# PSUM of a first stage shared out anew: three score buffers of two banks and two projection banks, for two and four

## The chip, the cores and the metric

The kernel runs on one core of a Trainium2 chip. The metric is the device time of one execution in microseconds (us), the median of several runs. All profile lines come from one profiled execution.

## What is computed

One layer reads x (4096 x 1024). A combined projection gives attention queries, a latent of 128 columns, indexer queries (8 heads of 32), indexer keys, head weights, gates, and the inputs of a state-space branch. The part that matters here is the choice of keys:

```python
idx_logits = jnp.einsum('bthd,bsd->bths', qi_b, ki)
index_score = jnp.einsum('bths,bth->bts', jax.nn.relu(idx_logits), wi_b)
index_score = jnp.where(causal[None], index_score, neg)
_, sel = lax.top_k(index_score, n_sel)          # n_sel = 256 of up to 4096 keys
```

Attention then runs over the chosen keys alone, the state-space branch is scanned, and both are gated, projected and normalised.

## The kernel before

The work falls into two halves. The **first stage** (lines 162 to 797) makes all projections and chooses the keys. The second (lines 801 to 1386: attention, state-space scan, output) needs the choice of all keys: a matmul (L1027) adds up a test over all groups, the result decides whether a slower selection has to run, and only then does attention begin.

In the first stage two kinds of work share the engines.

**Projections.** `prepare(c)` loads a chunk of 512 rows of x in eight tiles, transposes each with four PE instructions (L483) into a PSUM tile `ps_x`, and splits it in two (L85 on ACT, L87 on DVE; both read PSUM). `sweep(c, cols)` multiplies: one column block is 24 matmuls (eight triples, L98 to L100) into one `ps_x`, which ACT, or ACT and DVE, then drain. Indexer queries and keys need further short matmuls (L546, L547, L559 to L564), the keys and values of attention others; each takes a `ps_x` of its own. The weights of a sweep after the first are loaded by POOL's queue (L511).

**Selection.** The 30 query tiles that need a choice are taken in ten groups of two to five (`ORDER`); the last one is `[10, 11, 20, 21]`. `score(i)` makes the index scores of tile i: for each head, PE fills a `ps_i` of two banks with up to two matmuls (L254), ACT takes its relu into SBUF (L256), and DVE adds it with the head's weight to the tile's row of scores (L265). Then `select` searches a threshold in six or eight rounds. A round counts the scores above it, for some tiles on ACT (L325), for the others on DVE (L329), and is followed by 11 to 20 small DVE operations (L331 to L367). The first DVE operation of a group's rounds is L318, the first after them L372. Then each tile is cleaned up (L386 on ACT; L390, L391, the MAX8 of L393 and the MATCH_REPLACE8 of L401 on DVE) and its mask is written (L405). There are four large score buffers `acc`, so about two groups are in hand at once.

```python
165    psi = idxs.enter_context(tc.tile_pool(name="i_ps", bufs=2, space=PSUM))
251                    pi = psi.tile([P, 2 * C], FT, name="ps_i")
256                    ACT.activation(r[:, q0:q0 + m], pi[:, :m], AF.Relu)
457        pst = ph.enter_context(tc.tile_pool(name="p_t", bufs=4, space=PSUM))
481                ps = pst.tile([P, 4, P], FT, name="ps_x")
537                ps = pst.tile([P, C], FT, name="ps_x")
785        prepare(0)
786        for c in range(NCH):
787            sweep(c, range(3), None)
788            if c + 1 < NCH:
789                prepare(c + 1)
794        for g in ORDER:
795            select(g)
796        for c, following in zip((NCH - 1, *range(NCH - 1)), (*range(NCH - 1), None)):
797            sweep(c, range(3, len(COLS)), following)
```

PSUM has eight banks of 512 fp32 columns; `ps_i` takes two, `ps_x` one. So the program text has the three blocks one after the other, but it isn't the order in which they run: a scheduler with a model of the instructions' times orders each engine's queue when the program is built, and mixes projections of the last block (lines 796 and 797) in between the scores of the selection. Within a queue everything then runs in that fixed order: an instruction that waits holds up all behind it. In the second half the order on PE, DVE and ACT is written out by hand.

Of the kernel before, what the change touches and what calls it, by code (L numbers as in the profile page):

```python
# [27 lines left out]
PSUM = bass.MemoryType.PSUM  # L28
# [43 lines left out]
def tile_hymba(  # L72
# [89 lines left out]
    idxs = ctx.enter_context(ExitStack())  # L162
    one = idxs.enter_context(tc.tile_pool(name="i_one", bufs=1))
    wk = idxs.enter_context(tc.tile_pool(name="i_wk", bufs=2))
    psi = idxs.enter_context(tc.tile_pool(name="i_ps", bufs=2, space=PSUM))

    kst = one.tile([P, S], FR, name="kst")
    wi = one.tile([P, NT, HEADS], FT, name="wi")
# [284 lines left out]
    with ExitStack() as ph:  # L453
        xp = ph.enter_context(tc.tile_pool(name="p_x", bufs=1))
        wp = ph.enter_context(tc.tile_pool(name="p_w", bufs=WB))
        sm = ph.enter_context(tc.tile_pool(name="p_s", bufs=1))
        pst = ph.enter_context(tc.tile_pool(name="p_t", bufs=4, space=PSUM))

        selh = sm.tile([P, 4, P], FR, name="selh")
        sell = sm.tile([P, 4, P], FR, name="sell")  # L460
# [955 lines left out]
```

## Time and profile before

| | us |
|---|---|
| median of 3 runs (4113.29 to 4124.88) | 4118.75 |
| the profiled execution | 4111.49 |
| its span | 4109.7 |
| last score matmul of the selection starts (PE) | 1662.58 |
| the matmul that closes the first stage (L1027) | 1787.18 |

The rows below are of the profiled execution; times count from the start of its span. PEld is TensorE's weight load, PEclk the granted clock as a share of full speed. A wait is written as "who waited <- for whom".

### The profile page before, as it was taken

The page shows a single profiled execution, that of the slowest core. Times are in us where ns is not written, and L with a number is a line of the kernel's source. Part 1 is how long each engine was busy: PE and PEld are TensorE (multiplying, and loading weights), DVE is VectorE, ACT ScalarE, POOL GpSimd, SP SyncE. Part 2 cuts the span into 40 slices and gives each one's busy share as a digit, 9 for nine tenths or more (in the row PEclk, how much of TensorE's full clock was granted, in tenths as well). Part 3 has the DMA queues.
Part 4 walks back from the last instruction along what each step waited for, and adds up shares of the span by engine and source line. Part 5 has one row for each costly group of instructions (what it writes and reads, how often), then busy time and mean ns, then how long its engine had stood idle before and what let it go on. Part 6 is the DMA issues. An engine that isn't in the chain of part 4 may idle for free.

```text
span 4109.7 us, 64216 instructions
## 1 busy us (share of the span) xinstructions
PE 3683.6 (90%) x20925; PEld 3111.3 (76%) x20925; DVE 3298.1 (80%) x6879; ACT 2804.1 (68%) x4540; POOL 1545.4 (38%) x3405
## 2 busy tenths in 40 slices
PE   6788988988989989149999999999999999899998
PEld 5566766766757658038888898888898989788887
DVE  5898898888798888778888888888888889565554
ACT  4587878776767776647777777777777778534342
POOL 1110011111111111236665656666656542354543
PEclk9889989989989899569999999999999999999999
DMA  8766967767668677244545444444444444644441
GB/s 226 159 195 177 307 190 213 200 183 221 190 188 230 185 202 203 71 141 117 154 120 149 124 136 137 128 136 127 140 132 135 119 142 121 181 135 134 143 124 72
DMA packets 521898, 656.19 MB, mean 160 GB/s; under 512 B 126800, under 2 KB 367952, under 8 KB 521552
## 3 DMA queue, kind: packets, MB, share of 16 engines
q1 hardware_dynamic: 438800, 448.54, 37.7%
q0 software_dynamic: 82752, 203.45, 18.5%
q8 instruction: 167, 2.74, 0.3%
q14 instruction: 179, 1.47, 0.1%
HBM read 480.61 MB, written 169.13 MB: 158 GB/s over the span
## 4 chain that ended last, share of the span: by engine, by line
PE 45%; ACT 3%; DMA 3%; issue 2%; DVE 2%; POOL 2%; SPq 0%; ACTq 0%; POOLq 0%; DVEq 0%
PE ps_t L1149 10%; PE ps_o L1161 6%; PE ps_o L1162 5%; PE ps_s L1116 5%; PE ps_s L1117 5%; PE ps_y L99 2%; PE ps_y L98 2%; PE ps_y L100 2%; ACT sc L1132 2%; PE ps L959 2%; PE ps_g L99 1%; PE ps_g L100 1%; PE ps_g L98 1%; DMA mb<-mask_d 1%; ACT ph L85 1%
## 5 line engine op out<-in xcount | busy, mean ns | idle before, releaser
L87 DVE TENSOR_TENSOR pl<-ps_t,ph 128x512 fp32r<-128x512 f32 x1088 | 748.5, 689 | 194.2 <-ACT ph L85 181.1
L85 ACT ACTIVATE ph<-ps_t 128x512 fp32r<-128x512 f32 x1088 | 644.2, 596 | 372.6 <-PE ps_t L1149 353.8
L1119 DVE CUSTOM_DVE_ANT_0 sc<-ps_s,mb 128x512 f32<-128x512 f32 (+3 forms) x1152 | 725.6, 638 | 39.2 <-PE ps_s L1117 18.2
L1161 PE MATMUL ps_o<-ph,V 128*128 128x256 f32 x2176 | 659.3, 325 | 29.9 <-ACT ot L1165 27.0
L1149 PE MATMUL ps_t<-ident,sc 128*128 128x128 f32 x4352 | 655.7, 273 | 10.5 <-DVE pl L87 6.0
L256 ACT ACTIVATE relu<-ps_i 128x1024 f32<-128x1024 f32 (+5 forms) x624 | 534.6, 899 | 168.8 <-PE ps_i L254 147.2
L1132 ACT ACTIVATE sc<-sc,mx 128x1024 f32<-128x1024 f32 (+7 forms) x640 | 637.0, 997 | 7.3 <-DVE mx L1119 7.0
L1149 PEld LDWEIGHTS ps_t<-ident,sc 128*128 128x128 f32 x4352 | 537.0, 141 | 122.6 <-DVE pl L87 6.6
L265 DVE SCALAR_TENSOR_TENSOR acc<-relu,wi,acc 128x2048 f32<-128x2048 f32 (+15 forms) x322 | 558.1, 1733 | 77.2 <-ACT relu L256 74.3
L1162 PE MATMUL ps_o<-pl,V 128*128 128x256 f32 x2176 | 565.0, 282 | 2.6 <-DVE pl L87 2.6
L511 POOL DMA_DIRECT2D w<-w_d x294 | 159.0, 541 | 1085.9 <-PE ps_x L100 1005.8
L98 PE MATMUL ps_x<-xk,w 128*128 128x512 f32 x1280 | 517.1, 404 | 6.5 <-DVE st L87 2.0
L100 PE MATMUL ps_x<-xk,w 128*128 128x512 f32 x1280 | 507.3, 396 | 0.0
L99 PE MATMUL ps_x<-xk,w 128*128 128x512 f32 x1280 | 506.5, 396 | 0.0
L254 PE MATMUL ps_i<-kst,qst 128*128 128x512 f32 (+1 forms) x1136 | 394.9, 446 | 117.2 <-ACT relu L256 111.2
L1116 PE MATMUL ps_s<-KT,QH 128*128 128x512 f32 (+2 forms) x1152 | 438.2, 381 | 19.6 <-DMA V<-v_d 15.2
L1161 PEld LDWEIGHTS ps_o<-ph,V 128*128 128x128 f32 x2176 | 413.5, 190 | 47.4 <-ACT ot L1165 39.5
L1117 PE MATMUL ps_s<-KT,QL 128*128 128x512 f32 (+2 forms) x1152 | 436.4, 379 | 0.7 <-DVE QL L87 0.7
L1162 PEld LDWEIGHTS ps_o<-pl,V 128*128 128x128 f32 x2176 | 417.6, 192 | 7.3 <-DVE pl L87 3.3
L254 PEld LDWEIGHTS ps_i<-kst,qst 128*128 128x128 f32 x1136 | 222.1, 213 | 223.9 <-ACT relu L256 185.7
L325 ACT ACTIVATE junk_a<-acc,s_t 128x1920 int8<-128x1920 f32 (+14 forms) x152 | 333.1, 2191 | 53.8 <-DVE s_t L354 24.1
L98 PEld LDWEIGHTS ps_x<-xk,w 128*128 128x128 f32 x1280 | 245.7, 192 | 70.5 <-DMA w<-w_d 6.2
(408 smaller groups left out, 7435.4 us busy)
## 6 DMA issues: line engine op xcount, KB each, us to landing
w<-w_d POOLq DMA_DIRECT2D x294, 512.0 KB, 4.2
mb<-mask_d SPq DMA_DIRECT2D x416, 256.0 KB, 3.1
xs<-in_x_dram SPq DMA_DIRECT2D x120, 256.0 KB, 4.6
w_d<-w SPq DMA_DIRECT2D x42, 512.0 KB, 4.3
qs_d<-st SPq DMA_DIRECT2D x64, 256.0 KB, 3.0
k_d<-st SPq DMA_DIRECT2D x128, 128.0 KB, 2.4
v_d<-st SPq DMA_DIRECT2D x64, 256.0 KB, 3.5
QL<-qT_d SPq DMA_DIRECT2D x64, 256.0 KB, 4.2
```

The lines of the kernel that those rows point to most:

```text
L85: ACT.activation(hi, src, AF.Copy, scale=scale)
L87: DVE.tensor_tensor(lo, src, ft(hi), op=OP.subtract)
L98: PE.matmul(ps, lh, rh, start=first, stop=False)
L99: PE.matmul(ps, lh, rl, start=False, stop=False)
L100: PE.matmul(ps, ll, rh, start=False, stop=last)
L1116: PE.matmul(ps[:, :nn], QH[:, qs], kk, start=True, stop=False)
L1117: PE.matmul(ps[:, :nn], QL[:, qs], kk, start=False, stop=True)
L1119: DVE.tensor_tensor_reduce(self.sc[a][-1][:, o], ps[:, :n], self.mb[a][:, o], 1.0, TOP, OP.add, OP.min, mx[:, k:k + 1])
L1132: ACT.activation(v, v, AF.Exp, scale=-1.0, bias=nm, accum_out=self.ds[:, a, r:r + 1])
L1149: PE.transpose(pt[:, e, a, :], self.sc[a][r][:, o:o + P], ident)
L1161: PE.matmul(self.po, v, ph_[:, e, :], start=(b + e == 0), stop=False)
L1162: PE.matmul(self.po, v, pl_[:, e, :], start=False, stop=(b + e == self.nb - 1))
```

## The change

The pool of `ps_i` gets three buffers, and that of `ps_x` two. All eight banks are taken before (2 x 2 + 4) and after (3 x 2 + 2).

```diff
@@ -162,7 +162,7 @@
-    psi = idxs.enter_context(tc.tile_pool(name="i_ps", bufs=2, space=PSUM))
+    psi = idxs.enter_context(tc.tile_pool(name="i_ps", bufs=3, space=PSUM))
@@ -454,7 +454,7 @@
-        pst = ph.enter_context(tc.tile_pool(name="p_t", bufs=4, space=PSUM))
+        pst = ph.enter_context(tc.tile_pool(name="p_t", bufs=2, space=PSUM))
```

No instruction is added or removed, but the scheduler puts the first stage's queues in another order. Three places show it; `kst`, `qst`, `xk`, `w` are operands of the matmuls, `s_t`, `s_ab`, `s_e`, `s_d` the small vectors of the rounds.

PE, the last score of the last group, before:

```order
L254 MATMUL ps_i<-kst,qst 128x512
L254 MATMUL ps_i<-kst,qst 128x256
L98 MATMUL ps_x<-w,qh 128x512
L99 MATMUL ps_x<-w,qh 128x512
L100 MATMUL ps_x<-w,ql 128x512
L1027 MATMUL ps_i<-lo_14184,ones 1x11
```

And in the changed kernel:

```order
L98 MATMUL ps_x<-xk,w 128x512
L254 MATMUL ps_i<-kst,qst 128x512
L254 MATMUL ps_i<-kst,qst 128x256
L99 MATMUL ps_x<-xk,w 128x512
L100 MATMUL ps_x<-xk,w 128x512
L98 MATMUL ps_x<-xk,w 128x512
```

Before, three matmuls of projections stand between the last score and L1027; now 506 of them do. The longest run of other PE instructions between two scores was 92 long; now there are five of 117, 186, 230, 256 and 292 (1081 together) ahead of the last score.

DVE, the start of the last group's rounds (L318), before:

```order
L87 TENSOR_TENSOR st<-ps_x,st 128x512
L265 SCALAR_TENSOR_TENSOR acc<-relu,wi,acc 128x768
L318 TENSOR_TENSOR s_t<-zc,sdl 128x4
L337 TENSOR_TENSOR s_e<-sdl,gc 128x4
L319 TENSOR_TENSOR s_t<-s_t,s_mv 128x4
L265 SCALAR_TENSOR_TENSOR acc<-relu,wi,acc 128x768 x2
L87 TENSOR_TENSOR st<-ps_x,st 128x512
```

And in the changed kernel:

```order
L265 SCALAR_TENSOR_TENSOR acc<-relu,wi,acc 128x768
L350 RECIPROCAL s_e<-s_d 128x2
L318 TENSOR_TENSOR s_t<-zc,sdl 128x4
L351 TENSOR_TENSOR s_e<-s_e,s_ab 128x2
L337 TENSOR_TENSOR s_e<-sdl,gc 128x4
L319 TENSOR_TENSOR s_t<-s_t,s_mv 128x4
L352 TENSOR_SCALAR s_e<-s_e 128x2
```

The operations on `128x2` are rounds of the group before, `[22, 23]`: it had been finished when the last group began, and now has its last rounds and its clean-up still ahead. From L318 to the last tile's L401 DVE had 175 instructions and has 254. Those that came in: 12 of L87 (128x512), two of L329 (128x2944), two each of L393 and L401, four each of L390 and L391 (two 128x2048 each, the rest narrower), two of L265 (128x768), three more rounds of small operations, and a few others.

PE, the transposes (L483) for one chunk of the last sweeps, before:

```order
L483 MATMUL ps_x<-ident,xs 128x128 x6
L254 MATMUL ps_i<-kst,qst 128x512 x4
L483 MATMUL ps_x<-ident,xs 128x128 x12
L254 MATMUL ps_i<-kst,qst 128x512 x2
L483 MATMUL ps_x<-ident,xs 128x128 x4
```

And in the changed kernel:

```order
L99 MATMUL ps_x<-xk,w 128x512
L100 MATMUL ps_x<-xk,w 128x512
L483 MATMUL ps_x<-ident,xs 128x128 x32
L98 MATMUL ps_x<-qh,w 128x512
L99 MATMUL ps_x<-ql,w 128x512
```

Scores stood between the transposes of a chunk; now all eight tiles of this chunk stand in one row, over two banks. Of the 15 chunks that are prepared it is so, or nearly so, for about half.

## Rows read from the trace of the kernel before

**Rows 1.** Page, part 1: busy time, share of the span and instructions.

```profile
PE 3683.6 (90%) x20925; PEld 3111.3 (76%) x20925; DVE 3298.1 (80%) x6879; ACT 2804.1 (68%) x4540; POOL 1545.4 (38%) x3405
```

**Rows 2.** Stretches of the first stage, busy time of each engine in us.

```profile
core 0: us, PE busy (x) PEld busy (x) DVE busy (x) ACT busy (x) POOL busy (x), PEclk, DMA share, GB/s
170.00:1661.00 1491.00, 1317.87 (x5400) 1011.19 (x5398) 1284.01 (x2109) 1110.56 (x1388) 182.55 (x344) 0.92 0.73 204
767.00:900.00 133.00, 118.45 (x475) 88.62 (x474) 124.75 (x158) 101.27 (x119) 17.46 (x33) 0.91 0.72 203
900.00:953.00 53.00, 53.00 (x236) 43.45 (x235) 41.40 (x83) 40.85 (x38) 9.97 (x19) 1.00 0.79 218
1661.00:1780.00 119.00, 3.21 (x7) 1.33 (x5) 93.64 (x191) 67.13 (x75) 19.14 (x29) 0.50 0.18 56
```

**Rows 3.** Waits from 170 to 1661 us: total us, times, longest us.

```profile
ACT relu L256 <- PE ps_i L254: 123.4, 94, 4.6
PE ps_i L254 <- ACT relu L256: 107.7, 108, 6.1
DVE acc L265 <- ACT relu L256: 80.7, 65, 7.2
DVE s_t L331 <- ACT junk_a L325: 52.8, 25, 6.0
PE ps_x L98 <- DVE st L87: 22.6, 18, 3.4
PE ps_x L546 <- ACT st L549: 6.6, 1, 6.6
PE ps_x L483 <- DVE xk L87: 6.6, 5, 3.7
```

**Rows 4.** Timeline, PE after 1662 us, then DVE at 1661 us: start, duration.

```profile
1662.58 1.01 PE L254 MATMUL ps_i<-kst,qst 128*128 128x512 f32 x2 [1.01 <-ACT relu L256]
1666.37 0.63 PE L100 MATMUL ps_x<-w,ql 128*128 128x512 f32 x1
1787.18 0.20 PE L1027 MATMUL ps_i<-lo,ones 128*1 128x11 f32 x2 [120.18 <-DVE lo L1025]
...
1660.89 0.15 DVE L318 TENSOR_TENSOR s_t<-zc,sdl 128x4 f32<-128x4 f32 x1
```

**Rows 5.** Lines by form, DVE, 1600 to 1790 us: busy us, mean ns.

```profile
L391 DVE TENSOR_TENSOR acc<-acc,mk 128x2048 f32<-128x2048 f32 x4 | 9.1, 2287 | 0.0
L265 DVE SCALAR_TENSOR_TENSOR acc<-relu,wi,acc 128x768 f32<-128x768 f32 x7 | 7.1, 1009 | 2.0 <-ACT relu L256 1.9
L390 DVE TENSOR_SCALAR mk<-acc,s_t 128x2048 bf16<-128x2048 f32 x4 | 5.1, 1274 | 1.7 <-ACT acc L386 1.7
L329 DVE TENSOR_SCALAR_CACHE_REDUCE mk<-acc,s_t 128x2944 uint8<-128x2944 f32 x1 | 3.3, 3281 | 0.0
L393 DVE MAX8 s_top<-acc 128x8 f32<-128x2944 f32 x1 | 3.2, 3227 | 0.0
L401 DVE MATCH_REPLACE8 acc<-s_top,acc 128x3080 f32<-128x3080 f32 x1 | 3.4, 3350 | 0.0
L87 DVE TENSOR_TENSOR st<-ps_x,st 128x512 fp32r<-128x512 f32 x4 | 2.7, 685 | 0.1
```

**Rows 6.** Lines up to 1790 us: busy us, mean ns of one | idle before.

```profile
L325 ACT ACTIVATE junk_a<-acc,s_t 128x1920 int8<-128x1920 f32 (+14 forms) x152 | 333.1, 2191 | 53.8 <-DVE s_t L354 24.1 <-DVE s_t L361 14.0 <-DVE s_t L367 11.8
L329 DVE TENSOR_SCALAR_CACHE_REDUCE mk<-acc,s_t 128x512 uint8<-128x512 f32 (+9 forms) x72 | 202.2, 2808 | 1.6
L85 ACT ACTIVATE xk<-ps_x 128x512 fp32r<-128x512 f32 x120 | 69.8, 626 | 26.7 <-PE ps_x L483 26.3
L87 DVE TENSOR_TENSOR xk<-ps_x,xk 128x512 fp32r<-128x512 f32 x120 | 78.8, 681 | 18.8 <-ACT xk L85 18.2
```

**Rows 7.** Lines from 900 to 953 us: busy us, mean ns | idle before.

```profile
L265 DVE SCALAR_TENSOR_TENSOR acc<-relu,wi,acc 128x1792 f32<-128x1792 f32 x7 | 14.6, 2085 | 6.2 <-ACT relu L256 6.1
```

## The prediction, made before the changed kernel ran

> **What bounds the kernel now.** The page says which engines are loaded: PE 90%, DVE 80%, ACT 68% of the span [rows 1]. That is an average over two halves, and the change touches the first alone: in the second half the order is written by hand and other pools hold PSUM. The first stage ends with the matmul of L1027 at 1787.18 us [rows 4], so the question is how much earlier or later that one starts.
>
> The second view is the table of stretches [rows 2]. From 170 us (the first group's scores are there) to 1661 us (those of the last group nearly are), DVE is busy 1284.01 of 1491 us, 86.1%; ACT 1110.56, 74.5%. PE's 1317.87 us overstate it, since matmuls overlap: from 900 to 953 us it does 236 of them in 53 us without a pause, 0.225 us each, and 5400 at that rate are 1213 us, 81%. So DVE is nearest to being the bound, but none is one: the stage runs on waits between three in-order queues. Its best stretch, 767 to 900 us, has DVE at 124.75 of 133 us, 93.8%. After 1661 us comes a tail: PE has nothing left (its next matmul follows after 120.18 us idle [rows 4]), and DVE and ACT run the last group's rounds, DVE busy 93.64 of 119 us, 78.7%.
>
> The third view is the list of waits [rows 3]. ACT waits 123.4 us for scores of PE while PE, mostly, is busy with projections that stand ahead in its queue; PE waits 107.7 us for a free score buffer; DVE waits 80.7 us for relus. These are what a third buffer acts on. PE's waits for a free projection bank are small with four banks: 22.6 us, 6.6 us and 6.6 us in the three largest rows.
>
> **The change, term by term.** The sums are on the profiled execution, 4111.49 us, which is 7.26 us under the median of 4118.75 us; a difference is carried over to the median as it is. A difference under 0.3% (12 us) is about what a measurement of this kernel can't tell from none.
>
> *The tail.* In the new order, work that DVE did ahead of the last group's rounds stands behind their first operation, L318. Priced by [rows 5]: 12 x 0.685 = 8.2 us of splits; 2 x 3.281 = 6.6 of counts; L393 and L401, two each at about 3.3, 13.2; L391, 2 x 2.287 and about 1.15 for each of the two narrower ones, 6.9; L390, 2 x 1.274 and about 0.7 for each narrower one, 4.0; L265, 2 x 1.009 = 2.0; the small operations of three rounds, the group's threshold and some column scaling, about 50 at 0.15 us (one of them is L318 itself [rows 4]), 8. Together 49 us. At the body's 86.1% this is 57 us, so L318 moves from 1660.89 us to about 1604. The tail then has 93.64 + 49 = 143 us of DVE work where it had 94. At the tail's own share of 78.7% it would take 181 us and end at 1785, 5 us later than now; at the body's 86.1%, 166 us, 10 us earlier; at the best stretch's 93.8%, 152 us, 24 us earlier; with no idle at all, 33 us earlier. I take 90%, midway between body and best stretch: a second group's rounds and some splits fill the holes that one lonely chain of rounds leaves. That is 159 us, an end at 1763, **-17 us** (+5 to -33). PE's 506 projections behind the last score are 506 x 0.225 = 114 us; they start near 1606 and end near 1720 at full clock, some 45 us ahead of L1027: hidden, unless PE's waits for its two banks use that up. Projections on PE up to 1720 also shorten the stretch in which its clock is at half (0.50 in the tail), but in 1661 to 1780 us nothing waits for that clock.
>
> *The third score buffer.* PE may run one relu further ahead, so ACT's 123.4 us of waiting shrink. What reaches DVE is less: ACT is idle 1491 - 1110.56 = 380 us, and 123.4 of that (32%) is for scores; charging DVE's 80.7 us of relu waits in that ratio gives 26 us. The rest is ACT being late because it counts (a count takes 2.191 us [rows 6]), which no PSUM buffer cures. PE's 107.7 us are not a gain by themselves, since PE isn't the bound. Bounds 0 and -26; I take half, **-13 us**, since the scores are now also issued in denser bursts, at the end of which PE meets the same full buffers.
>
> *Two projection banks.* For a column block, 24 matmuls x 0.225 = 5.4 us fill one bank while the other is drained in 0.626 and 0.681 us [rows 6]: cost 0 unless the drain is queued behind a count. For the transposes a tile is filled in 4 x 0.225 = 0.9 us and drained in 1.31 us; with two banks six of the eight tiles wait some 0.4 us, 2.5 us a chunk, 37 us over 15 chunks. If each pair of tiles has to sit out one count on ACT and one on DVE (2.191 + 2.808 us [rows 6]), it is 15 us a chunk, 225 us in all. These are waits of PE; a wait ahead of ACT has so far reached DVE as 26 of 123 us, 0.21. So +8 to +47 us. I take **+8**: the order leaves scores between the transposes of about half the chunks, and has 243 us of pure projection on PE (below) in which it isn't hurried.
>
> *Bursts.* Ahead of the last score the 1081 instructions in long runs between scores are about 243 us in which DVE gets no relus and lives on rounds and splits. The nearest stretch is 900 to 953 us, when two groups count at once and PE is full of projections: DVE at 41.40 of 53 us, 78%. Were all 243 us like this instead of at 86.1%, it would cost 243 x (1 - 0.78/0.861) = 23 us. But 6.2 us of that stretch's idle time is waiting for relus [rows 7], which a stretch without scores can't have; without it the share is 41.40 of 46.8 us, 88%. I take **0**, between 0 and +23.
>
> The Trainium skill, "Perfetto Trace Analysis", section Optimization Strategy, says that where the busiest engine changes over time it may pay to interleave the regimes; the new order does the opposite. By that rule the bursts would be a loss, and the sum -22 + 23, about nothing; the 88% speaks against it as far as one stretch can.
>
> **Sum:** -17 - 13 + 8 + 0 = **-22 us**: 4089 us for the profiled execution, **4097 us** for the median.
>
> **The rivals.**
>
> *A. Slower: PE stalls on two banks.* Place: the transposes of L483, eight tiles in one row, and the short matmuls of L546 and L547 in groups of four. PE is in order, so a transpose that waits for a drain behind a count holds up the scores behind it; ACT and then DVE run dry. For it: half of the chunks have lost the scores in between, and drains do queue behind counts (today's longest waits for L87 are 3.4 and 3.7 us [rows 3]). Against it: with four banks the waits are small, and PE has about a fifth of its time free. It decides once PE's waits on `ps_x` pass some 150 us, up from 36: 150 x 0.21 = 31 us, more than the tail gives, and with half of the bursts' 23 us and no gain from the buffer the sum is -17 + 31 + 12 = +26 us, 4145 us; up to -17 + 47 + 23 = +53 at the bounds.
>
> The same skill page, section Optimizing Tensor Performance, wants independent groups of matmuls to rotate through banks so that a drain overlaps the next group's matmuls. By it, fewer banks for the many short groups is the wrong way; the 0.9 against 1.31 us above is where it bites here.
>
> *B. No difference.* DVE's work isn't changed by a single instruction; if relu waits only turn into waits at other places, and the tail runs at 83% rather than 90%, the terms are within 12 us of nothing: 4107 to 4131 us. For it: DVE's other waits, such as 52.8 us for ACT's counts [rows 3], stay.
>
> *C. Much faster.* If most of the 80.7 us go, because counts on ACT no longer leave DVE dry with two full buffers waiting, and the tail closes up as well: -24 - 45 + 8 = about -61 us, 4058 us. For it: the long wait rows on both sides of `ps_i`. Against it: a relu still has to pass ACT.
>
> **How the numbers follow.** The forecast (12 to 45 us faster) gets 0.42; C 0.12; B 0.21; A 0.25. Hence faster by over 0.3%: 0.54; within: 0.21; slower: 0.25. The point is the forecast's, 4097 us. The range reaches down past C's middle to 4045 us and up past A's to 4150 us, leaving about 1 in 10 out on either side. The faster cases alone would lie between 4045 and 4107 us.
>
> **What would show it.** Right: L318 of the last group near 1600 us and L1027 near 1765; projections on PE until about 1720; ACT's wait for L254 well under 100 us; DVE's for relus near 65. Wrong: PE's waits on `ps_x` (L483, L546, L98) adding up to over 150 us would mean A; DVE's busy share from 170 us to the last L318 unchanged at 86%, and a tail of over 175 us, would mean B. The second half should last as long as before; if it doesn't, the argument has missed something outside the stage.

## The result and the profile after

The changed kernel takes **4222.59 us** (median of five runs, 4218.51 to 4226.29); the kernel before takes 4118.75 us (five runs, 4113.29 to 4124.88). The ratio is **1.0258**, 95% interval 1.0242 to 1.0274: slower by some 104 us. The prediction said 4097 us, faster, with a range up to 4150 us. Its sign is wrong, and its range misses the time.

The profiled execution has a span of 4220.7 us, against 4109.7 us before. Page, part 1, of the changed kernel, which answers to [rows 1]:

```profile
PE 3757.9 (89%) x20925; PEld 3133.6 (74%) x20925; DVE 3290.4 (78%) x6879; ACT 2808.4 (67%) x4540; POOL 1544.0 (37%) x3405
```

Each engine does as many instructions as before, and DVE and ACT are busy equally long within 0.3%. So the 111 us of span came in as waiting, and as slower matmuls on PE (its busy time rises by 74.3 us at the same count). Where it came in is read off the starts of a few landmarks. The view of one line gives, for the first and the last of them, the stores of attention's output (L1166), before and then after:

```profile
L1166 SPq DMA_DIRECT2D o_d<-ot x128: 319/320/1377, 1821.9 to 3527.4; - x128
```

```profile
L1166 SPq DMA_DIRECT2D o_d<-ot x128: 319/320/1162, 1926.3 to 3636.0; - x128
```

The third field holds the shortest, median and longest duration in ns, then come the first and the last start in us. From first to last store it is 1705.5 us before and 1709.7 us after, so the attention loop itself lasts nearly as long as it did (4.2 us more). Its first store comes 104 us later. So nearly all of the loss lies ahead of 1926 us.

The timeline of the changed kernel (start, duration) answers to [rows 4]: the last group's start on DVE, the last score, the last L401, and the matmul with which the stage ends.

```profile
1631.69 0.17 DVE L318 TENSOR_TENSOR s_t<-zc,sdl 128x4 f32<-128x4 f32 x1 [0.86 <-POOL sdl L307]
1641.28 0.52 PE L254 MATMUL ps_i<-kst,qst 128*128 128x512 f32 x2
1798.98 3.08 DVE L401 MATCH_REPLACE8 acc<-s_top,acc 128x2824 f32<-128x2824 f32 x1
1819.53 0.20 PE L1027 MATMUL ps_i<-lo,ones 128*1 128x11 f32 x2
1819.76 0.16 DVE L1028 CAST lo<-ps_i 1x11 int32<-1x11 f32 x1 [8.46 <-PE ps_i L1027]
```

The last L401 of the kernel before:

```profile
1776.66 3.08 DVE L401 MATCH_REPLACE8 acc<-s_top,acc 128x2824 f32<-128x2824 f32 x1
```

The selection ends 22 us later than before (its last L401 started at 1776.7 us, now at 1799.0), L1027 comes 32 us later (before at 1787.18), and attention's first store 104 us later: the loss grows in three steps. At the end of the stage it is DVE that waits, 8.46 us, for PE, which still had projections ahead of L1027 in its queue. From L1027 to the first store it is 34.7 us before and 106.8 us now.

**How the first 1100 us look.** The table of stretches (columns as in [rows 2]), before and then after:

```profile
170.00:1100.00 930.00, 815.99 (x3368) 624.02 (x3367) 803.96 (x1368) 714.34 (x938) 102.57 (x192) 0.92 0.74 207
```

```profile
170.00:1100.00 930.00, 747.45 (x2879) 547.01 (x2880) 797.87 (x1379) 691.62 (x902) 90.85 (x158) 0.86 0.62 175
```

DVE nearly keeps its pace (797.87 us busy after 803.96). PE does not: 2879 matmuls instead of 3368, **489 fewer**, at a granted clock of 0.86 of full speed instead of 0.92. PE is idle 182.6 us instead of 114.0, which is 68.5 us more, and a matmul takes 0.2596 us of its busy time instead of 0.2423, which over 2879 of them is 50 us. Together that is 118.5 us, which is another way of writing 489 matmuls at 0.2423 us. Score matmuls (L254) alone in the same stretch (PE, PEld, clock, DMA share, GB/s), before and then after:

```profile
170.00:1100.00 930.00, 234.64 (x680) 130.96 (x680) 0.92 0.74 207
```

```profile
170.00:1100.00 930.00, 240.87 (x684) 133.72 (x685) 0.86 0.62 175
```

The scores are on time, so what went undone by 1100 us is projections, and they have to be done later. PE's queue has a fixed order, so how many projections stand ahead of a given score was settled when the program was built: the new order puts fewer there. From 1100 to 1640 us DVE does fall behind a little, with 448.55 us busy after 463.20.

The waits from 170 to 1661 us after, the same stretch as [rows 3]:

```profile
PE ps_i L254 <- ACT relu L256: 109.9, 119, 8.5
DVE s_t L331 <- ACT junk_a L325: 87.5, 28, 10.5
ACT relu L256 <- PE ps_i L254: 67.1, 44, 3.2
DVE acc L265 <- ACT relu L256: 51.4, 43, 3.6
PE ps_x L483 <- DVE xk L87: 46.3, 27, 5.2
ACT relu L256 <- DVE acc L265: 44.8, 38, 8.2
PE ps_x L98 <- DVE st L87: 35.8, 18, 9.5
PE ps_x L98 <- DVE xk L87: 10.0, 7, 4.7
PE ps_x L546 <- ACT st L549: 8.2, 3, 7.8
```

Two things happened. The third score buffer did what it was argued to do: ACT's wait for scores fell from 123.4 to 67.1 us and DVE's for relus from 80.7 to 51.4 us. But ACT now waits 44.8 us for DVE to take a relu (5.6 us before), and DVE 87.5 us for ACT's counts (52.8 before): what was gained on one side of the two engines is given back on the other. And PE waits for projection banks, above all the transposes of L483, 46.3 us instead of 6.6. All PE waits ahead of an instruction on `ps_x` sum to 137.8 us in this stretch, against 63.5 us before; up to 1790 us to 217.2 us in 154 waits, against 103.6 us in 82, with some 30 to 35 us in each that are waits for loads and the like.

**How attention starts.** Of the projections, 543 stand between the last score and L1027 in PE's queue (506 of L98 to L100, and 37 transposes and other short ones), and another **156 behind** the branch that opens the attention part; before, 3 and none. After, every 25 us from 1815 us:

```profile
1815.00:1840.00 25.00, 16.39 (x61) 11.95 (x59) 1.38 (x2) 2.74 (x4) 6.68 (x12) 0.88 0.79 198
1840.00:1865.00 25.00, 17.52 (x70) 14.38 (x71) 0.00 (x0) 1.20 (x2) 6.04 (x7) 0.78 0.76 242
1865.00:1890.00 25.00, 16.11 (x55) 11.42 (x53) 6.83 (x20) 7.77 (x16) 3.67 (x15) 0.80 0.74 223
1890.00:1915.00 25.00, 4.89 (x9) 2.50 (x9) 4.70 (x12) 3.66 (x9) 9.57 (x18) 0.54 0.80 232
1915.00:1940.00 25.00, 20.90 (x131) 18.41 (x132) 17.26 (x53) 16.78 (x37) 24.28 (x40) 0.85 0.43 115
```

Before, the attention loop was at its pace by 1830 us, 43 us after its L1027:

```profile
1830.00:1855.00 25.00, 24.81 (x175) 22.11 (x174) 23.05 (x64) 19.74 (x42) 14.50 (x43) 1.00 0.45 117
```

For 70 us after L1027 hardly anything of attention moves: DVE is busy 1.38, 0.00 and 6.83 us of 25. Before, it was busy 23.05 us of 25 from 43 us after L1027 on. What each engine waits for there (after, 1820 to 1926 us):

```profile
DVE sc L1119 <- DMA mb<-mask_d: 38.8, 1, 38.8
ACT st L597 <- PE ps_x L100: 35.1, 4, 20.5
PE ps L875 <- POOL M L846: 18.5, 1, 18.5
POOL V L953 <- PE ps_x L100: 14.0, 1, 14.0
PE ps_x L98 <- DMA w<-w_d: 8.4, 1, 8.4
```

Attention's first score on DVE (L1119) stands 38.8 us for a mask. The mask's load (L1101, on SP's queue) first starts at 1871.2 us, and at 1796.2 us before: on SP it stands behind stores of leftover projections, which wait for ACT (L597), which waits for PE. Behind the last of the 156, which ends at 1900.4 us, PE waits 18.5 us at L875, a matmul of the state-space branch, for a matrix that POOL makes (L846); POOL itself had waited 14.0 us for the last projection (L953). So leftovers on PE hold up four other queues: ACT, SP, DVE and POOL.

### The profile page after: what moved, and what is told of

It is laid out like the page before. It is cut to its first block, busy times and chain, and to the rows that moved or that the text cites. A ratio compares the mean times of both kernels' runs of the same rounds, so it can differ in the third digit from the quotient of the medians.

```text
span 4220.7 us, 64409 instructions
## 1 busy us (share of the span) xinstructions
PE 3757.9 (89%) x20925; PEld 3133.6 (74%) x20925; DVE 3290.4 (78%) x6879; ACT 2808.4 (67%) x4540; POOL 1544.0 (37%) x3405
## 4 chain that ended last, share of the span: by engine, by line
PE 54%; DVE 7%; issue 6%; ACT 6%; DMA 5%; POOL 3%; SPq 0%; DVEq 0%; POOLq 0%; ACTq 0%
PE ps_t L1149 9%; PE ps_o L1161 5%; PE ps_o L1162 5%; PE ps_s L1116 5%; PE ps_s L1117 5%; PE ps_x L98 3%; PE ps_x L99 3%; PE ps_x L100 3%; PE ps_y L99 2%; PE ps_y L100 2%; PE ps_y L98 2%; DVE acc L265 2%; DMA w<-w_d 2%; ACT sc L1132 2%; PE ps L959 2%
## 5 line engine op out<-in xcount | busy, mean ns | idle before, releaser
L87 DVE TENSOR_TENSOR pl<-ps_t,ph 128x512 fp32r<-128x512 f32 x1088 | 749.0, 689 | 197.5 <-ACT ph L85 183.9
L85 ACT ACTIVATE ph<-ps_t 128x512 fp32r<-128x512 f32 x1088 | 643.5, 596 | 373.2 <-PE ps_t L1149 355.7
L1119 DVE CUSTOM_DVE_ANT_0 sc<-ps_s,mb 128x512 f32<-128x512 f32 (+3 forms) x1152 | 726.3, 639 | 71.4 <-DMA mb<-mask_d 47.2
L265 DVE SCALAR_TENSOR_TENSOR acc<-relu,wi,acc 128x2048 f32<-128x2048 f32 (+15 forms) x322 | 560.5, 1741 | 49.6 <-ACT relu L256 46.5
L98 PE MATMUL ps_x<-xk,w 128*128 128x512 f32 x1280 | 522.1, 408 | 48.4 <-DMA w<-w_d 17.6
L254 PE MATMUL ps_i<-kst,qst 128*128 128x512 f32 (+1 forms) x1136 | 400.5, 456 | 126.1 <-ACT relu L256 110.6
L100 PE MATMUL ps_x<-xk,w 128*128 128x512 f32 x1280 | 508.6, 398 | 0.6 <-DVE w L507 0.6
L254 PEld LDWEIGHTS ps_i<-kst,qst 128*128 128x128 f32 x1136 | 223.6, 217 | 240.2 <-ACT relu L256 192.8
L325 ACT ACTIVATE junk_a<-acc,s_t 128x1920 int8<-128x1920 f32 (+14 forms) x152 | 332.6, 2188 | 40.8 <-DVE s_t L354 23.3
L98 PEld LDWEIGHTS ps_x<-xk,w 128*128 128x128 f32 x1280 | 247.7, 194 | 125.2 <-issue 18.9
```

What stands on the lines that cost most here:

```text
L87: DVE.tensor_tensor(lo, src, ft(hi), op=OP.subtract)
L98: PE.matmul(ps, lh, rh, start=first, stop=False)
L100: PE.matmul(ps, ll, rh, start=False, stop=last)
L265: DVE.scalar_tensor_tensor(o, r, wi[:, i, h:h + 1], more, op0=OP.mult, op1=OP.add)
L1119: DVE.tensor_tensor_reduce(self.sc[a][-1][:, o], ps[:, :n], self.mb[a][:, o], 1.0, TOP, OP.add, OP.min, mx[:, k:k + 1])
```

## The experiments

Theory: with two banks PE has a backlog of projections at the last score, while the selection nearly keeps its pace, and pays at the end, partly ahead of L1027 and partly behind the branch; the third score buffer does nothing either way. Rivals: the third score buffer is itself the loss; the transposes' drains behind counts are the place; or DVE loses inside the selection. A backlog "N/M" below is the number of PE instructions between last score and L1027, and that of projections behind the branch; both can be read off the order before a run. Ratios are to the kernel before, timed beside each run (4105.92, 4104.73 and 4105.82 us for runs 1 to 4, 5 to 8 and 9 to 11).

### 1 and 2. Two score buffers; two or three projection banks

```diff
@@ e1: line 165 as before, line 457
-        pst = ph.enter_context(tc.tile_pool(name="p_t", bufs=4, space=PSUM))
+        pst = ph.enter_context(tc.tile_pool(name="p_t", bufs=2, space=PSUM))
@@ e2: the same with bufs=3
```

> Two score buffers as before, two projection banks as after (two of the eight banks unused). In its order 192 projection matmuls stand behind the branch that ends the first stage (156 in the changed kernel, none before). Theory 1 (the two projection banks cost the time): as slow as the changed kernel, 4190 to 4250 us. Theory 2 (the third score buffer costs it, because scores run ahead and push projections back): close to the kernel before, 4110 to 4150 us.

> Two score buffers, three projection banks. In its order no projection stands behind the branch, 100 stand between the last score and it. Theory 1: most of the loss goes, since what costs is the work left over behind the branch: 4100 to 4150 us. If instead each missing bank costs its own share of waits on PE, half of the loss stays: about 4170 us. Theory 2: as before, 4105 to 4135 us.

Two banks: 4205.53 us, **1.0240** (1.0222 to 1.0257), backlog 386/192. Three banks: 4133.35 us, **1.0061** (1.0044 to 1.0077), backlog 100/0. With two score buffers in all three kernels, the loss goes 0, 0.6%, 2.4% as banks go 4, 3, 2. The stretch up to 1100 us of the kernel with three banks:

```profile
170.00:1100.00 930.00, 787.24 (x3163) 590.23 (x3161) 792.33 (x1338) 699.79 (x918) 96.89 (x177) 0.91 0.67 194
```

Matmuls done by 1100 us: 3368, 3163, and 2916 with two. Taking away two banks alone reproduces almost all of the loss: 1.0240 and the changed kernel's 1.0258 have overlapping intervals.

Two banks and three do not lose in the same place. With two banks the selection ends no later than before, and the loss comes all behind it (last L401, first store of attention):

```profile
1774.23 3.08 DVE L401 MATCH_REPLACE8 acc<-s_top,acc 128x2824 f32<-128x2824 f32 x1
```

```profile
L1166 SPq DMA_DIRECT2D o_d<-ot x128: 319/320/1407, 1906.5 to 3614.2; - x128
```

With three banks the 100 projections left are done by 1726.4 us, while the rounds still run, and PE then idles 84 us; its selection ends 23 us late (1803.1 us), its first store comes 22 us late. So its 0.6% is not the price of a backlog, and why its selection is late isn't shown. Its time, 4133.35 us, is also inside the range of theory 2.

### 3. The changed kernel with no leftovers behind the branch

Two small operations on DVE (L539 and L605 here) read results of the last projections and make the branch wait for them, so that the program's order puts all projections ahead of it. Lines after 204 move by two, after 535 by four, after 599 by six, and from 1013 on by four again.

```diff
+    lost = one.tile([P, NT], FT, name="lost")
+    DVE.memset(lost, 0.0)
...
+                            if following is None and e > 3 and a == 3 and r == 1:
+                                DVE.tensor_scalar(lost[:, 1:2], ft(st)[:, 0, 0:1], 0.0, None, op0=OP.mult)
...
+                    if following is None and n == "gs" and j == 3:
+                        DVE.tensor_scalar(lost[:, 0:1], st[:, 0:1], 0.0, None, op0=OP.mult)
...
-    lost = one.tile([P, NT], FT, name="lost")
...
-    DVE.memset(lost, 0.0)
```

> The changed kernel, with the test that ends the first stage made to wait for the last projections too (a zero made from each of the last two results is written into two unused places of it): the order ahead of it stays, and nothing is left behind the branch. If the place behind the branch costs more than the work itself (attention's first steps and the projections wait for each other in the in-order queues), L1027 starts some 40 to 55 us later than in the changed kernel but attention runs at full pace at once: 4170 to 4200 us. If it is only the work that is late, the time stays at 4210 to 4235 us.

4191.52 us, **1.0205** (1.0188 to 1.0222), backlog 699/0. Against 1.0258 that is 0.5%, 22 us, for the 156 behind the branch. The rest, 84 us, stays. It comes ahead of the branch now: the last score is at 1635.5 us, L1027 (here L1031) at 1866.0 us, 79 us later than before, and the first output store at 1901.9 us, 80 us later than before. The tail in four pieces, and the longest wait of DVE in it:

```profile
1640.00:1700.00 60.00, 49.17 (x216) 38.89 (x214) 47.27 (x96) 37.58 (x43) 8.65 (x17) 0.91 0.74 232
1700.00:1750.00 50.00, 26.37 (x72) 17.12 (x71) 33.61 (x94) 37.15 (x49) 2.11 (x4) 0.60 0.45 127
1750.00:1800.00 50.00, 46.24 (x199) 36.97 (x199) 41.66 (x73) 28.14 (x31) 8.84 (x17) 1.00 0.81 241
1800.00:1866.00 66.00, 51.90 (x205) 38.44 (x204) 10.18 (x55) 11.25 (x22) 9.62 (x24) 0.87 0.82 236
```

```profile
DVE lost L605 <- ACT st L601: 41.0, 1, 41.0
```

The 699 instructions would take 699 x 0.225 = 157 us at the full rate and take 225 us, to 1860.7 us. From 1700 to 1750 us PE does 72 in 50 us, at a clock of 0.60, while ACT and DVE are busy with the selection's rounds. Once those are over (the last L401 here ends at 1794.9 us) DVE stands 41.0 us for a drained block (L605), and then drains the last projections until 1863.9 us: PE ends the stage.

### 4. One score buffer, six projection banks

```diff
-    psi = idxs.enter_context(tc.tile_pool(name="i_ps", bufs=2, space=PSUM))
+    psi = idxs.enter_context(tc.tile_pool(name="i_ps", bufs=1, space=PSUM))
...
-        pst = ph.enter_context(tc.tile_pool(name="p_t", bufs=4, space=PSUM))
+        pst = ph.enter_context(tc.tile_pool(name="p_t", bufs=6, space=PSUM))
```

> One score buffer, six projection banks: what a score buffer is worth by itself. Every relu then waits for its matmuls and they for the relu before. If the third buffer had nothing to give because two already suffice, the loss from two to one is what shows: 624 relus with 0.5 us of matmuls not hidden, up to 300 us of ACT's time, of which a fifth reaches DVE: 4160 to 4250 us. If score buffers hardly matter: 4110 to 4140 us.

4721.68 us, **1.1493** (1.1470 to 1.1516), far outside both ranges. Its waits up to 2400 us:

```profile
ACT relu L256 <- PE ps_i L254: 589.1, 417, 8.0
PE ps_i L254 <- ACT relu L256: 537.5, 391, 6.8
DVE acc L265 <- ACT relu L256: 482.4, 183, 12.2
```

With one buffer a score can only be made while no relu reads: both sides wait for each other and DVE runs dry for 482.4 us. No backlog arises here; the selection itself is late (its last L318 at 2272.0 us). So the curve of the score buffers is steep from one to two (if the two more projection banks cost nothing, which wasn't tried), and the next run shows it flat from two to three, at two projection banks.

### 5 and 6. Two score buffers and two banks, nothing behind the branch; the changed kernel again

The edit of 3 on the kernel of 1; and the changed kernel as it is, timed beside it.

> Run 1 (two score buffers, two projection banks) with the end of the first stage waiting for the last projections, as in run 3; nothing is left behind the branch. Against run 3 (4191.5 us, 1.0205 of the kernel before) it shows the third score buffer alone, at two banks and without the work left over. If the third buffer costs by pushing projections back (run 3 has 699 projections after the last score, this one 578, 121 fewer at 0.225 us): 1.014 of the kernel before, 4165 us. If it does nothing: within 0.2% of run 3.

> The changed kernel once more, for a comparison with runs 1 and 5 on one chip. Third buffer without effect: within 0.2% of run 1's ratio of 1.0240. Third buffer a loss of its own: 1.026 or more.

The first: 4191.86 us, **1.0207** (1.0193 to 1.0221), the same as with three score buffers (1.0205); its L1031 starts at 1865.2 us, there at 1866.0. The changed kernel again: 4210.98 us, 1.0256 (1.0242 to 1.0270). So at two projection banks the third score buffer by itself is worth nothing that can be measured, with or without leftovers behind the branch (1.0240 against 1.0256). With four projection banks there is no room for it.

### 7 and 8. Draining the transposes on ACT alone

If the transposes' two drains, one on ACT and one on DVE (L85, L87), hold the banks behind DVE's counts, then letting ACT copy the tile out twice takes DVE out of the bank's way. DVE then splits from SBUF. It costs ACT 120 copies of about 0.6 us [rows 6], 72 us; the control has the same edit with four banks and two score buffers.

```diff
-                split(xk[:, 0], xk[:, 1], ps.rearrange("p a t -> p (a t)"))
+                flat = xs.rearrange("p a t -> p (a t)")
+                ACT.activation(xk[:, 0], ps.rearrange("p a t -> p (a t)"), AF.Copy)
+                ACT.activation(flat, ps.rearrange("p a t -> p (a t)"), AF.Copy)
+                DVE.tensor_tensor(xk[:, 1], flat, ft(xk[:, 0]), op=OP.subtract)
```

> The changed kernel, with the bank of a transposed tile released without DVE: ACT reads it twice (the rounded part, and a copy into the tile's own input buffer), and DVE subtracts in SBUF. 120 more ACT copies of about 0.6 us, 72 us of ACT's time. If the transposes' wait for DVE (62 us of PE's waits) is a main part of what two banks cost, L483's waits fall to 20 us or less, fewer projections are left, and a third of the loss goes: 4170 to 4195 us. If the transposes matter little, the copies only cost: 4225 to 4260 us.

> Control for run 7: the same edit in the kernel before, with four banks, where PE hardly waits for a transposed tile's bank. What it costs here is the price of the 120 copies: 4106 to 4130 us by the theory that DVE, not ACT, is nearest to the bound; above 4140 us if ACT is.

On the changed kernel 4207.28 us, **1.0242** (1.0226 to 1.0258), backlog 559/108; the control 4165.17 us, **1.0139** (1.0124 to 1.0155). The first lies between its two ranges; the second falls in the branch by which ACT is nearest to the bound. Waits of the first from 170 to 1640 us (its lines after 484 have moved by three):

```profile
PE ps_x L98 <- DVE st L87: 72.2, 22, 9.5
PE ps_x L483 <- DMA xs<-in_x_dram: 30.2, 14, 5.4
PE ps_x L483 <- ACT xs L487: 17.4, 31, 2.1
```

The transposes' wait for DVE (46.3 us) is gone, 17.4 us for ACT's copies stand in its place, but the wait of the column blocks for DVE doubled (35.8 to 72.2 us), and the input tiles, which are now held longer, let PE wait for loads (30.2 us). PE does 2901 matmuls up to 1100 us, as many as in the changed kernel. Relieving one user of the two banks moved the wait to the other. The control shows why this pair can't settle which user matters: its 72 us of copies on ACT cost 60 us of time, with DVE's wait for relus, both to 1640 us, up from 78.5 to 110.9 us. The edit also changes the order of the queues.

### 9 to 11. Fewer projection matmuls

If the loss is PE's undone work, less of that work should shrink it. In the blocks of `q`, `ga`, `gs` and `u` the product of the weights' high part with the inputs' low part is left out, 1024 matmuls in all (1024 x 0.225 = 230 us of PE); the outputs lack that product. The same cut on the changed kernel, on the kernel before, and on the kernel of 1:

```diff
+                    if n in ('ga', 'gs', 'q', 'u'):
+                        PE.matmul(ps, w[k // 4][:, 0, k % 4, :], xc[k][:, 0], start=k == 0, stop=False)
+                        PE.matmul(ps, w[k // 4][:, 1, k % 4, :], xc[k][:, 0], start=False, stop=k == KD - 1)
+                        continue
```

> The changed kernel with less work for PE: the 16 column blocks of queries, gates and state-space inputs leave out the product with the low part of x, so their blocks have 16 matmuls in place of 24 (1024 matmuls fewer, 230 us at 0.225 us each; no bank is filled or drained less often, and ACT and DVE do all they did). In its order 144 projections stand after the last score and none behind the branch. Backlog theory (two banks slow PE down, and what it has not done by the last score sets the end): most of the loss goes, 4105 to 4145 us. If the loss comes from late drains on ACT and DVE, which are as many as before: above 4170 us.

> Control for run 9: the same cut in the kernel before, which has no backlog. PE isn't its bound, so 230 us less of PE work should give little: 4070 to 4110 us. If PE is a bound there too, most of it shows: under 4020 us.

> The same cut with two score buffers and two projection banks: beside run 9 it shows what the third score buffer gives where PE's projections no longer set the end. If it is worth what its waits suggest (ACT waits 40 us less for scores, DVE 28 us less for relus): run 9 is 10 to 30 us faster than this one. If it is worth nothing: within 0.2%.

Measured: 4157.82 us, **1.0123** (1.0098 to 1.0147), backlog 144/0; the control with four banks 4175.53 us, **1.0152** (1.0122 to 1.0182), backlog 0/0; two and two 4164.33 us, **1.0125** (1.0098 to 1.0151), backlog 208/0. On the changed kernel the cut gives back 1.3%, and its first output store comes at 1867.5 us instead of 1926.3. Nothing is left behind the branch. Yet 4157.82 us lies between its two ranges (up to 4145, above 4170), so the expectation was missed; e11 is within the 0.2% of e9 that means a third score buffer without effect. Against the control the two-bank kernels are no slower any more. But the control missed too: 230 us less work on PE made the kernel with four banks 1.5% slower, and its expectation was a gain or nothing. Its waits from 170 to 1640 us:

```profile
PE ps_i L254 <- ACT relu L256: 159.8, 120, 36.8
PE ps_x L540 <- DMA w<-w_d: 51.7, 65, 2.3
PE ps_x L98 <- DVE st L87: 50.1, 19, 9.0
```

and its second stretch, beside the same stretch of the kernel before:

```profile
1100.00:1640.00 540.00, 381.16 (x1355) 267.33 (x1354) 435.98 (x679) 363.08 (x411) 99.24 (x159) 0.80 0.64 185
```

```profile
1100.00:1640.00 540.00, 487.25 (x1984) 376.80 (x1983) 463.20 (x721) 384.03 (x434) 77.60 (x147) 0.92 0.72 202
```

PE meets weight tiles that aren't there yet (51.7 us on the shortened line; 1.8 us for weights before), one score waits 36.8 us for a buffer, the clock is 0.80 instead of 0.92, and DVE does less in the same time (435.98 against 463.20 us). Which of these comes first, and whether it is the new order that the cut gives rise to, isn't settled. What 9 to 11 do show stands in the next table.

### All kernels by two landmarks

From each profiled execution, in us: the end of the selection (of the last L401) and the first store of attention. Backlogs as above.

| kernel: score buffers, projection banks | backlog | selection ends | first store | between |
|---|---|---|---|---|
| before: 2, 4 | 3/0 | 1779.7 | 1821.9 | 42.2 |
| changed: 3, 2 | 543/156 | 1802.1 | 1926.3 | 124.2 |
| changed again (e6) | 543/156 | 1791.5 | 1913.4 | 121.9 |
| e1: 2, 2 | 386/192 | 1777.3 | 1906.5 | 129.2 |
| e2: 2, 3 | 100/0 | 1803.1 | 1843.9 | 40.8 |
| e3: 3, 2, all ahead of the branch | 699/0 | 1794.9 | 1901.9 | 107.0 |
| e4: 1, 6 | 0/0 | 2384.4 | 2425.1 | 40.7 |
| e5: 2, 2, all ahead of the branch | 578/0 | 1786.9 | 1902.3 | 115.4 |
| e7: 3, 2, ACT drains | 559/108 | 1800.7 | 1914.9 | 114.2 |
| e8: 2, 4, ACT drains | 0/0 | 1833.8 | 1874.8 | 41.0 |
| e9: 3, 2, fewer matmuls | 144/0 | 1825.4 | 1867.5 | 42.1 |
| e10: 2, 4, fewer matmuls | 0/0 | 1842.3 | 1887.2 | 44.9 |
| e11: 2, 2, fewer matmuls | 208/0 | 1842.5 | 1879.9 | 37.4 |

A backlog of up to 208 is done while the last rounds run, and the two landmarks are 37 to 45 us apart, as before. One of 578 to 699 puts them 107 to 129 us apart. Taking matmuls out brings the two-bank kernels back from 124 and 129 to 42 and 37 us, so the backlog's price is gone there, as the theory says. What e9 to e11 lose is the selection itself, 46 to 63 us late, and why it is late isn't settled. By how much the selection is late differs by 11 us between two executions of the changed kernel.

**No version ran faster than the kernel before.**

## Why the prediction was wrong, point by point

**What bounds the kernel.** The prediction took DVE as nearest to the bound and read PE's load (81% at the full rate) as slack. It put the difference to PE's 1317.87 busy us down to overlapping matmuls, but the clock in the same row accounts for it: 1213 us at full clock are 1318 us at the granted 0.92, by the same estimate. At the clock it had, PE was busy 88% of the stretch, more than DVE, and free for 173 us, not 278. And PE's projections are a fixed amount of work that has to be finished within the stage, in a queue without overtaking. Slack on such an engine is what it has until the end, and the prediction spent it twice: on waits for two banks and on a tail full of projections.

**"Two projection banks", +8 (to +47): the step that failed.** Its place was right (L483, in rows of eight tiles; and L98), and the wait rose as its mechanism said, from 6.6 to 46.3 us. The step priced PE's waits by what reaches DVE at the time, 0.21 of them. Little reached DVE at the time: its busy time changed from 803.96 to 797.87 us up to 1100 us and from 463.20 to 448.55 us between 1100 and 1640 us, and in e1 the selection ended no later than before (1777.3 us after 1779.7). What was lost stayed on PE as undone projections, 489 matmuls by 1100 us, 699 at the last score, and came due at the end: 82 us more from the end of the selection to attention's first store, and 87 us in e1. Measured for two banks alone: e1, 1.0240, which is 99 us. (e2, one bank less, loses 0.61% or 25 us, but without a backlog to pay.)

**"The tail", -17.** L318 moved from 1660.89 to 1631.69 us (forecast 1604), and from there to the end of the last L401 it took 170 us (forecast 159), so the selection ended 22 us late instead of 17 early. That the 170 us come so near is luck: DVE's work in it was 131 us, not 143, at a share of 77%, not 90% (130.58 of 170 us from 1632 to 1802 us). The holes that a second group's rounds and splits were to fill stayed: 77% is about the share of the old tail, 78.7%. The larger failure, by the time it cost, is in the sentence that called 506 projections hidden until about 1720 us at 0.225 us each. They weren't done at that rate: 543 took from 1641 to 1820 us, 178 us instead of 122. PE stood idle for 41.8 us of it, some 30 us of that for drains and other results of DVE and ACT, which were in their rounds, and the clock was at 0.88 (stretch from 1640 to 1820 us). The prediction had named this risk ("unless PE's waits for its two banks use that up") and given it no price. In e3 the whole backlog stands ahead of the branch; that kernel is 84 us slower, and the table gives 65 us of it to the time behind the selection and 15 to a selection that ends later.

**"The second half should last as long as before."** Attention's loop nearly did (1709.7 against 1705.5 us). Its start did not: the prediction overlooked the 156 projections that stand behind the branch, though the order, fixed when the program is built, has them there. Their place behind it cost 22 us by e3 against the changed kernel, and 14 us by e5 against e1.

**"The third score buffer", -13.** The waits fell nearly as forecast (relu waits "near 65" were 51.4 us, L254's "well under 100" were 67.1), but the time didn't: e3 against e5, 1.0205 and 1.0207. A relu that is there earlier found DVE busy (44.8 us of waiting on ACT), and counts on ACT were later (87.5 us). The bound of 0 was the value, at two projection banks.

**"Bursts", 0.** DVE's share from 170 us to the last L318 is 1242.91 of 1462 us, 85.0%, after 86.1%. The difference is worth some 16 us: inside the bounds (0 to +23), but more than the 12 us that the prediction calls nothing. How much of it is due to the bursts the runs don't show.

**Rivals.** A (slower, 0.25) had the right resource and the right rows, and the sum of `ps_x` waits came near its 150 us in the stretch of [rows 3] (137.8 us) and passed it up to 1790 us (217.2 us). It failed in the way to the time: it had PE's stall starve ACT and then DVE, which would cost 26 us, up to 53. The route was a debt of PE instead, and that has no factor of 0.21. B and C fell. Both sentences on the Trainium skill, "Perfetto Trace Analysis", spoke against the change. What its section Optimizing Tensor Performance says of rotating groups of matmuls through banks agrees with e1, where two banks for four cost 2.4%. What its section Optimization Strategy says of interleaving no run here shows, since none separates the bunching from the banks.

**Summed up.** Of some 104 us up to attention's first store, 82 lie behind the end of the selection and are the backlog on PE; 22 are a later end of the selection (12 and 80 in e6, -2 and 87 in e1). Of the backlog's price, 14 to 22 us are due to its place behind the branch (e5 against e1, e3 against the changed kernel). The third score buffer is worth about 0 (e5 against e3).

**What stays open.** The order of the program is fixed when it is built, and it changed with the number of banks. The size of the backlog is part of that order: in a queue without overtaking, waits at run time can't change what stands behind the last score. What the waits for banks at run time add (112.2 against 38.8 us of `ps_x` waits up to 1100 us) wasn't separated from the order: no kernel with the new order and four banks was tried, nor one with the old order and two. Which user of the banks, transposes or column blocks, weighs most isn't settled by e7, nor why the selection of e2 and of e9 to e11 is late.

## What to carry to other kernels

When buffers are moved from one user to another, price the loser by what its engine still has to do before the stage ends, not by the stall that its partner sees at the time: an in-order engine with "20% of its time free" can have work put off in silence and present the bill at a barrier. Count in the new order what it has left when its partner's last input is made, and whether that fits beside the partner's last steps (208 matmuls did here, 578 did not). Read the new order to the end, past the branch: work of the old stage among the first steps of the next one holds up more queues than its own. And move buffers one step at a time: here the score side gains nothing from two to three (at two projection banks) and loses 15% from two to one, the projection side loses 0.6% from four to three and 1.8% more to two.

## What the runs showed of the hardware that was not expected

- Waiting costs PE twice. Up to 1100 us the longer idle time is 68.5 us, and at a granted clock of 0.86 after 0.92 the matmuls that were done took 50 us more. From 1700 to 1750 us of e3 PE was busy 26.37 of 50 us at a clock of 0.60, and in the next 50 us, nearly without waits, 46.24 us at 1.00.
- 120 copies more on ACT, 72 us, cost 60 us (e8), though ACT is busy 74.5% of the stage against DVE's 86.1% [rows 2]. Longer-held input tiles and the order, which the edit changes too, may have a part in that.
- Less matmul work is not always less time: 1024 matmuls fewer left the kernel with four banks 1.5% slower (e10), with the clock at 0.80 from 1100 to 1640 us and the selection's end 63 us late. The cause isn't shown.
